# Up projections token-major, turned back through VectorE squares and DRAM

## The chip, the cores and the metric

One core of a Trainium2 chip runs the whole program. TensorE (PE) multiplies, VectorE (DVE) and ScalarE (ACT) do elementwise work, GpSimd (POOL) does little here, and the queues of SyncE (SP), ACT and POOL issue DMAs. The metric is device microseconds for one execution; the lower the better. A change of about 0.2% can be told from none.

## The reference

A decoder trunk of two layers over 256 tokens with D = 2048: a gated linear attention layer, then a block-sparse attention layer, each followed by the feed-forward block that the change touches:

```python
def conv_ffn(x, norm_w, w_up, conv_w, conv_b, w_down):
    h = rms_norm(x, norm_w) @ w_up              # (256, 2 * 5632)
    hp = jnp.pad(h, ((0, 0), (2, 0), (0, 0)))
    acc = conv_b
    for j in range(3):
        acc = acc + conv_w[j] * hp[:, j:j + S]  # causal, along the tokens, per feature
    a, u = jnp.split(acc, 2, axis=-1)
    return (jax.nn.silu(a) * u) @ w_down
```

All is float32.

## The kernel before

**Products.** A float32 product is made of three passes in the reduced type fp32r. Weights w are split into a high part (ACT's cast, line 132) and a low part (DVE's subtraction, line 133); the activations xw hold high and low parts side by side, 256 tokens each. A product is high x high, high x low and low x high, all summed in PSUM.

**Steps.** The program is an unrolled list of steps. In each step one 128x1024 piece of weights is taken from `WeightStream` and multiplied. `WeightStream` loads 128x2048 chunks (1 MB, three buffers `wraw`) through SP's queue (line 95) and splits them two steps or a little more ahead into three buffer pairs `whi`, `wlo`. `after(n, job)` puts a job n steps later into the program's order. Within each engine, the order is then settled by a scheduler at build time, which keeps dependencies and waits for buffers.

**Two forms of projection.** `gemm` is feature-major: weights stand in the array (128x128), the tokens stream. Per 128x128 weight tile it runs a matmul of 512 columns (high weights against high and low tokens, line 291) and one of 256 (low weights against high tokens, line 293). Its result has features on the partitions and tokens along the row. `gemm_tok` is token-major: 128 tokens stand in the array and 512 weight columns stream (lines 306 and 309). Its result has tokens on the partitions. The attention projections of the second layer use `gemm_tok`.

**The up stage** (`ffn`), for each of 44 tile pairs j (128 columns of a and the matching 128 of u): `gemm` in four steps, then `both` adds the two halves of the PSUM result (ACT line 319, DVE line 320), the row of norm factors `nrm.rstd` is multiplied in (line 593), and the convolution runs along the tokens (ACT line 597, DVE lines 599 and 601), then silu (line 603), the product (line 604) and the split into `hid` (lines 327 and 328). For some tile pairs (`EARLY`) the sums that the down projection wants are made at once (`combine`, lines 551 to 554); for others they are made in the down stage (`combine_parts`, line 561).

**The down stage** (`down`) runs a Strassen-like scheme: where its order list has a `+`, seven products take the place of eight, with weight sums (lines 105 to 107) and activation sums (`comb`). Its last entries (behind the `|`) are the tail.

**Buffers.** `slot` hands out 34 buffers of 4 KB a partition for xw (8), hid (22), combinations, weight sums and the rest.

**The norm.** `Norm.close` gives one factor per token with tokens on partitions (`col`); `spread` turns it into a row over tokens with a diagonal and two matmuls. `middle` makes the input of an up stage: `back` transposes the finished rows on PE.

Of the kernel before, what the change touches and what calls it, by code (L numbers as in the profile page):

```python
# [8 lines left out]
F32 = mybir.dt.float32  # L9
F32R = mybir.dt.float32r  # L10
I32 = mybir.dt.int32
AF = mybir.ActivationFunctionType
# [6 lines left out]
S = 256  # L19
KT = D // 128  # L20
# [7 lines left out]
FT = F // 128  # L28
# [3 lines left out]
C_GN, C_KVN, C_MN, C_FN, C_ON, C_KN, C_QN, C_CW = 0, 16, 32, 48, 80, 84, 85, 86  # L32
# [8 lines left out]
    return [(int(k.rstrip("+")), k.endswith("+")) for k in words], len(text.split("|")[1].split())  # L41


EARLY = (1, 3, 5, 7)
ORDERS = {
    "go": [_order("0 1+ 2 3+ 4 | 5 6 7"), _order("0 2 1+ 3+ 4 | 5 6 7")],
    "dn0": [_order("0 2 4 1+ 6 3+ 8 5+ 10 7+ 12 9+ 14 11+ 16 13+ 17 15+ 18 | 19 20 21"),
# [10 lines left out]
class WeightStream:  # L58
# [4 lines left out]
    def __init__(self, tc, raw, parts):  # L63
        self.tc, self.nc, self.raw, self.parts = tc, tc.nc, raw, parts
        self.chunks, self.halves = [], []
        self.tiles, self.split = {}, {}
        self.n_dma = self.n_split = 0
        self.cuts, self.lead, self.deep = {}, {}, set()
        self.sums, self.slot, self.first = {}, None, None
# [79 lines left out]
def trunk(ctx: ExitStack, tc: tile.TileContext, xT, x_tok, cst, msk, w1p, w2a, w_k, w_qa, w_v2, w_v, w_g, w_go,  # L149
          w_up0, w_dn0, w_kk, w_kv, w_mq, w_mo, w_up1, w_dn1, rel, onehot, out):  # L150
    nc = tc.nc
    V, A, T = nc.vector, nc.scalar, nc.tensor
# [6 lines left out]
    small = ctx.enter_context(tc.tile_pool(name="small", bufs=2))  # L159
    acc_ps = ctx.enter_context(tc.tile_pool(name="acc_ps", bufs=3, space=PSUM))  # L160
    mis_ps = ctx.enter_context(tc.tile_pool(name="mis_ps", bufs=2, space=PSUM))
    dram = ctx.enter_context(tc.tile_pool(name="dram", bufs=1, space=DRAM))
# [10 lines left out]
    def acc_pair():  # L173
# [2 lines left out]

    ws = WeightStream(tc, raw, parts)
    plan = [(w_v2, 1, 16384), (w_v, 2, 8192), (w_k, 4, 4096), (w_qa, 4, 4096), (w_g, 8, 4096), (w_go, "go", None),
            (w_up0, FT, 4096), (w_dn0, "dn0", None),
            (w_mq, 4, 8192), (w_kk, 4, 8192), (w_kv, 4, 8192), (w_mo, "mo", None),  # L180
            (w_up1, FT, 4096), (w_dn1, "dn1", None)]
    for w, groups, cols in plan:
        if cols is None:
            for g, order in enumerate(ORDERS[groups]):
# [49 lines left out]
    ident = mk[:, 0:128]  # L234
# [37 lines left out]
    def after(steps, job):  # L272
        later.append((cur[0] + steps, job))
# [10 lines left out]
    def gemm(xs, kts):  # L284
        ps = acc_ps.tile([128, 2, 512], F32, name="acc")
        for q0 in range(0, kts, 4):
            hi, lo = step()
            for bs in ((0,), (1,)) if q0 == kts - 4 else ((0, 1),):
                tiles_ = [(q0 + k, b, k * 256 + b * 128) for k in range(4) for b in bs]
                for kt, b, c in tiles_:  # L290
                    T.matmul(ps[:, b, :], hi[:, c:c + 128], xs(kt), start=kt == 0, stop=False)  # L291
                for kt, b, c in tiles_:
                    T.matmul(ps[:, b, :S], lo[:, c:c + 128], xs(kt)[:, :S], start=False, stop=kt == kts - 1)  # L293
        ws.prefetch(cur[0])
        return ps
# [21 lines left out]
    def both(ps, name):  # L317
        t = temp(name)
        A.copy(t, ps[:, :, S:])
        V.tensor_add(t, t, ps[:, :, :S])  # L320
        return t

    def bc(r):
        return r[:, None, :S].to_broadcast([128, 2, S])
# [5 lines left out]
    class Norm:  # L330


        def __init__(self, c, name, along=False):
            self.c, self.name, self.along, self.xs = c, name, along, []
            self.ss = small.tile([128, 2, 4], F32, name="ss_n")

        def operand(self, p, src):
# [5 lines left out]
        def close(self):  # L343
            m = small.tile([128, 2], F32, name="m_n")
            self.col = small.tile([128, 2], F32, name="col_n")
            V.tensor_reduce(m, self.ss, axis=AX.X, op=OP.add)
            V.tensor_scalar(m, m, 1.0 / D, EPS, op0=OP.mult, op1=OP.add)
            nc.gpsimd.tensor_tensor(self.col, m, mhalf[:, :2], op=OP.pow)

        def spread(self):  # L350

# [9 lines left out]
    nrm = Norm(C_GN, "xw")  # L361
# [9 lines left out]
    xs = rows(nrm.xs)  # L371
# [81 lines left out]
    for hd in (2, 3):  # L453
        ps = gemm_tok(xs)
# [9 lines left out]
    for hd in range(GH):  # L464
        ps = gemm(xs, KT)
        rstd = nrm.rstd
        k = both(ps, "k")
        V.tensor_mul(k, k, bc(rstd))
        b = bcum[hd]
# [64 lines left out]
    for hd in range(GH):  # L534
        ps = gemm(xs, KT)
        q = both(ps, "q")
# [10 lines left out]
    def combine(k, halves_, into):  # L547

        (a0, a1), (b0, b1) = halves_
        t = temp("comb", (128, 4, 128))  # L550
        V.tensor_add(t[:, 0], a1, b1)
        V.tensor_sub(t[:, 1], t[:, 0], a0)
        V.tensor_sub(t[:, 2], a0, a1)
        V.tensor_sub(t[:, 3], b0, t[:, 1])
        c = slot([128, 4, 2, 128], F32R, "comb")
        split(c[:, :, 0], c[:, :, 1], t)
        into[k] = c
# [10 lines left out]
    for hd in range(GH):  # L568
        for c in range(2):
            ps = gemm(xs, KT)  # L570
# [13 lines left out]
    def ffn(layer, nrm, then):  # L584
        xs = rows(nrm.xs)
        hid, sums = [], {}
        whole = [None, None]
        cw = C_CW + layer * 3 * 2 * FT
        cb = C_CB + layer * 2 * FT
        for j in range(FT):  # L590
            ps = gemm(xs, KT)
            t = both(ps, "up")
            V.tensor_mul(t, t, bc(nrm.rstd))  # L593
            au = temp("au")
            for i in range(2):
                n = i * FT + j
                A.activation(au[:, i, :], t[:, i, :], AF.Identity, bias=col(cb + n),  # L597
                             scale=col(cw + 2 * 2 * FT + n))
                V.scalar_tensor_tensor(au[:, i, 1:], t[:, i, :S - 1], col(cw + 2 * FT + n), au[:, i, 1:],
                                       op0=OP.mult, op1=OP.add)  # L600
                V.scalar_tensor_tensor(au[:, i, 2:], t[:, i, :S - 2], col(cw + n), au[:, i, 2:],  # L601
                                       op0=OP.mult, op1=OP.add)
            A.activation(au[:, 0, :], au[:, 0, :], AF.Silu)
            V.tensor_mul(au[:, 0, :], au[:, 0, :], au[:, 1, :])
            if j % 2 == 0:
                hid.append(slot([128, 2, 2 * S], F32R, "hid"))
            split(hid[-1][:, j % 2, :S], hid[-1][:, j % 2, S:], au[:, 0, :])
            whole[j % 2] = (au[:, 0, :128], au[:, 0, 128:])
            if j % 2 and j // 2 in EARLY:
                combine(j // 2, whole, sums)  # L610
        then(hid, sums)

    def down(name, xs, combos, res, done, jobs):
# [73 lines left out]
    def onward(nrm, keep_row, parked=None):  # L687

        sums = {}

        def done(t, c, x):
            sums[t, c] = x
            nc.gpsimd.dma_start(keep_row(t, c), x)
            nrm.square(t, c, x)

        def back(q, where):
            tp = where()
            for i in range(2):
                for t in range(2):
                    f = 128 * (q % 2 * 2 + i)  # L700
                    T.transpose(tp[:, i, 128 * t:128 * t + 128], sums[t, q // 2][:, f:f + 128], ident)  # L701
            nrm.operand(q, tp)
            if parked is not None:
                x = temp("hf")
                A.copy(x, tp)
                nc.gpsimd.dma_start(parked[q], x.rearrange("a b c -> a (b c)"))

        pair = []

        def in_acc():  # L710
            if not pair:
                pair.extend(acc_pair())
            return pair.pop(0)

        def in_bank():
            return bank("hf", (128, 2, S))

        return done, back, in_acc, in_bank

    def middle(name, xs, combos, res, nrm, keep_row, at, feature_major, parked=None):  # L720
        done, back, in_acc, in_bank = onward(nrm, keep_row, parked)
        jobs = {}
        for q, (b, i) in enumerate(at):
            jobs.setdefault(b, {}).setdefault(i, []).append(lambda q=q: back(q, in_acc))
        down(name, xs, combos, res, done, jobs)
        for q in range(len(at), NP):
            after(1 if feature_major else q - 3, lambda q=q: back(q, in_bank))
        after(2 if feature_major else 3, nrm.close)
        if feature_major:
            after(3, nrm.spread)  # L730

    rows1, rows2, rows3 = scratch("rows1"), scratch("rows2"), scratch("rows3")
    hspill = dram.tile([NP, 128, 2 * S], F32, name="hspill")
# [7 lines left out]

        down("dn1", hid, sums, rows3, done, {})

    n_ffn = Norm(C_FN, "xw")
    middle("go", go, go_sums, from_input, n_ffn, rows1, TURNS, True)
    n_q = Norm(C_MN, "xw")
    ffn(0, n_ffn, lambda hid, sums: middle("dn0", hid, sums, rows1, n_q, rows2,
# [120 lines left out]
    xs = rows(n_q.xs)  # L868
    for g in range(4):
        ps = gemm_tok(xs)  # L870
# [4 lines left out]
        f = (q8[:, g % 2 * 4:g % 2 * 4 + 4], (q1[:, 0:2], q1[:, 2:4]))  # L875
# [22 lines left out]
        for c in range(2):  # L898
            after(1 + c, lambda v=v, p=2 * g + c: values(v, p))

    n_ffn = Norm(C_FN + KT, "xw")
    middle("mo", ox, {}, rows2, n_ffn, rows3, TURNS, True)
    ffn(1, n_ffn, last_down)

# [1 line left out]
def _chunks(w):  # L906
    import numpy as np
    g, _, n = w.shape
    full = n // 2048 * 2048
    body = w[:, :, :full].reshape(g, 128, full // 2048, 2048).transpose(0, 2, 1, 3).reshape(g, -1)  # L910
    return np.ascontiguousarray(np.concatenate([body, w[:, :, full:].reshape(g, -1)], axis=1))


def _groups(w, width):
    k, n = w.shape
    return _chunks(w.reshape(k // 128, 128, n // width, width).transpose(2, 1, 0, 3)
                   .reshape(n // width, 128, -1))
# [20 lines left out]

def _pairs(w):
    k, n = w.shape  # L940
    j = n // 256
    return _chunks(w.reshape(k // 128, 128, 2, j, 128).transpose(3, 1, 0, 2, 4).reshape(j, 128, -1))


def _buckets():
# [64 lines left out]
```

## Time and profile before

| | |
|---|---|
| median of 3 runs | 2233.89 us (2233.52 to 2234.81) |
| profiled execution, span | 2230.9 us (for this execution the span is what the page states; the median lies 3.0 us above it) |
| PE / DVE / ACT busy | 2214.3 / 1663.1 / 1278.0 us |
| DMA | 441.07 MB, mean 198 GB/s; SP's queue 54.1% of the 16 engines |
| granted TensorE clock | 0.9 or more of full speed in every fortieth of the span |
| first up stage | PE's up matmuls from 387.3 to 881.0 us |

Busy time counts an engine's instructions from start to end; PE's matmuls overlap, so the distance between starts tells more than durations. A group row gives count, busy us, mean ns of one instruction, then idle time before it and what ended that idle time. A window row gives busy us (and instructions) of each engine within a stretch, the granted clock, the share of the 16 DMA engines and GB/s.

### The profile page before, as it was taken

The numbers are of one execution on the slowest core, as the hardware profiler recorded it, in microseconds if no ns is written. First come the engines' busy times: TensorE is split into PE (matmuls) and PEld (weight loads), VectorE is DVE, ScalarE is ACT, GpSimd is POOL, SyncE is SP. The second block draws the span as 40 slices with busy tenths as digits, with TensorE's granted clock in tenths as the row PEclk, the third lists the DMA queues.
The fourth block names the chain that finished last, engine by engine and source line by source line (L and its number), as shares of the span: only waits on it lengthen the run. The fifth ranks groups of instructions, "written<-read, shape, count | busy, mean of one in ns | idle before, by whom it ended". The sixth has DMA issues, their size and how long they took to land.

```text
span 2230.9 us, 30027 instructions
## 1 busy us (share of the span) xinstructions
PE 2214.3 (99%) x11525; PEld 1892.1 (85%) x11525; DVE 1663.1 (75%) x2305; ACT 1278.0 (57%) x1803; POOL 81.0 (4%) x104
## 2 busy tenths in 40 slices
PE   9999999999999999999999999999999999999999
PEld 7889887888888888888878888778888888888877
DVE  6566787777777778978766666677777777779786
ACT  6556655555555555655456665556555555556553
POOL 1000001000000000010030000010000000000000
PEclk9999999999999999999999999999999999999999
DMA  8553567555555555575675544575555555555755
GB/s 315 172 188 131 189 218 233 180 187 188 188 188 188 188 189 198 187 256 202 221 282 201 170 159 162 200 229 179 187 189 188 189 189 189 188 196 186 240 208 170
DMA packets 69777, 441.07 MB, mean 198 GB/s; under 512 B 8273, under 2 KB 8801, under 8 KB 19586
## 3 DMA queue, kind: packets, MB, share of 16 engines
q1 hardware_dynamic: 60578, 417.53, 54.1%
q0 software_dynamic: 8480, 21.05, 3.7%
q8 instruction: 90, 1.47, 0.3%
q10 hardware_dynamic: 576, 0.58, 0.1%
q14 instruction: 53, 0.43, 0.1%
HBM read 428.61 MB, written 10.51 MB: 197 GB/s over the span
## 4 chain that ended last, share of the span: by engine, by line
PE 96%; DMA 2%; DVE 2%; issue 0%; ACT 0%; SPq 0%; DVEq 0%; ACTq 0%
PE acc L291 34%; PE acc L293 18%; PE acc L639 16%; PE acc L306 10%; PE p L639 10%; PE acc L309 5%; DVE wlo L133 1%; DMA wraw<-w_dn 1%; PE sT L504 0%; DMA wraw<-w_v 0%; PE tr L793 0%; PE acc L701 0%; PE s L811 0%; PE pT L831 0%; DMA wraw<-w_mo 0%
## 5 line engine op out<-in xcount | busy, mean ns | idle before, releaser
L133 DVE TENSOR_TENSOR wlo<-wraw,whi 128x1024 fp32r<-128x1024 f32 (+1 forms) x786 | 929.9, 1191 | 395.2 <-ACT whi L132 373.2
L132 ACT CAST whi<-wraw 128x1024 fp32r<-128x1024 f32 (+1 forms) x786 | 798.8, 1026 | 690.4 <-PE acc L291 392.1
L291 PE MATMUL acc<-xw,whi 128*128 128x512 f32 x3328 | 853.9, 393 | 0.0
L291 PEld LDWEIGHTS acc<-xw,whi 128*128 128x128 f32 x3328 | 591.0, 189 | 99.0
L293 PEld LDWEIGHTS acc<-xw,wlo 128*128 128x128 f32 x3328 | 468.1, 190 | 41.8
L293 PE MATMUL acc<-xw,wlo 128*128 128x256 f32 x3328 | 481.5, 282 | 0.0
L639 PE MATMUL acc<-whi,hid 128*128 128x512 f32 x572 | 182.4, 390 | 0.7 <-DVE c L680 0.7
L639 PE MATMUL p<-whi,hid 128*128 128x512 f32 x506 | 166.1, 389 | 0.0
L306 PE MATMUL acc<-whi,xkv 128*128 128x512 f32 x512 | 133.6, 394 | 0.0
L306 PE MATMUL acc<-whi,xw 128*128 128x512 f32 x512 | 129.1, 392 | 3.0 <-ACT xw L244 1.5
L132 ACT CAST whi<-t 128x1024 fp32r<-128x1024 f32 x82 | 86.2, 1052 | 77.6 <-PE p L639 48.9
L639 PEld LDWEIGHTS acc<-whi,hid 128*128 128x128 f32 x572 | 107.0, 188 | 23.1 <-DVE c L680 1.1
L306 PEld LDWEIGHTS acc<-whi,xw 128*128 128x128 f32 x512 | 95.0, 188 | 24.7 <-ACT whi L132 2.8
L639 PE MATMUL acc<-whi,comb 128*128 128x512 f32 x328 | 107.5, 391 | 4.6 <-ACT whi L132 3.0
L639 PEld LDWEIGHTS p<-whi,hid 128*128 128x128 f32 x506 | 95.0, 188 | 19.8
L133 DVE TENSOR_TENSOR wlo<-t,whi 128x1024 fp32r<-128x1024 f32 x82 | 99.7, 1220 | 13.7 <-ACT whi L132 8.0
L306 PEld LDWEIGHTS acc<-whi,xkv 128*128 128x128 f32 x512 | 94.3, 188 | 18.4
L597 ACT ACTIVATE au<-up,cs 128x256 f32<-128x256 f32 x176 | 96.4, 595 | 20.0 <-DVE up L593 20.0
L639 PE MATMUL acc<-wlo,hid 128*128 128x512 f32 x286 | 94.7, 390 | 0.5 <-DVE wlo L133 0.5
L639 PE MATMUL p<-wlo,hid 128*128 128x512 f32 x253 | 83.5, 389 | 0.0
L601 DVE SCALAR_TENSOR_TENSOR au<-up,cs,au 128x254 f32<-128x254 f32 x176 | 77.4, 478 | 0.0
L639 PEld LDWEIGHTS acc<-whi,comb 128*128 128x128 f32 x328 | 61.5, 188 | 18.2 <-ACT whi L132 3.7
(261 smaller groups left out, 2062.8 us busy)
## 6 DMA issues: line engine op xcount, KB each, us to landing
wraw<-w_up SPq DMA_DIRECT2D x176, 1024.0 KB, 4.9
wraw<-w_dn SPq DMA_DIRECT2D x88, 1024.0 KB, 5.0
wraw<-w_g SPq DMA_DIRECT2D x16, 1024.0 KB, 4.9
wraw<-w_go SPq DMA_DIRECT2D x16, 1024.0 KB, 5.4
wraw<-w_mq SPq DMA_DIRECT2D x16, 1024.0 KB, 5.6
wraw<-w_kk SPq DMA_DIRECT2D x16, 1024.0 KB, 4.9
wraw<-w_kv SPq DMA_DIRECT2D x16, 1024.0 KB, 4.9
wraw<-w_mo SPq DMA_DIRECT2D x16, 1024.0 KB, 4.9
```

The lines of the kernel that those rows point to most:

```text
L132: nc.scalar.copy(hi[:, a:b], src[:, a:b])
L133: nc.vector.tensor_sub(lo[:, a:b], src[:, a:b], hi[:, a:b].bitcast(F32))
L291: T.matmul(ps[:, b, :], hi[:, c:c + 128], xs(kt), start=kt == 0, stop=False)
L293: T.matmul(ps[:, b, :S], lo[:, c:c + 128], xs(kt)[:, :S], start=False, stop=kt == kts - 1)
L306: T.matmul(ps[:, t, :], xs(kt)[:, x0 + 128 * t:x0 + 128 * t + 128], hi[:, c:c + 512], start=kt == 0 and x0 == 0, stop=False)
L309: T.matmul(ps[:, t, :], xs(kt)[:, 128 * t:128 * t + 128], lo[:, c:c + 512], start=False, stop=kt == KT - 1)
L597: A.activation(au[:, i, :], t[:, i, :], AF.Identity, bias=col(cb + n), scale=col(cw + 2 * 2 * FT + n))
L601: V.scalar_tensor_tensor(au[:, i, 2:], t[:, i, :S - 2], col(cw + n), au[:, i, 2:], op0=OP.mult, op1=OP.add)
L639: T.matmul(p[n], x[xi], w[wi][:, 512 * f:512 * f + 512], start=n not in begun, stop=left[n] == 0)
```

## The change

Both up stages go from `gemm` to `gemm_tok`: 22 groups J of 512 columns (a and u of two tile pairs) instead of 44 pairs of 256. The weights are laid out for it on the host. The result has tokens on the partitions, so it is turned back: ACT takes it out of PSUM with the norm factor of each token as scale; DVE transposes each 32x32 square; SP stores the squares to a DRAM scratch (one DMA of 512 KB, contiguous runs of 1 KB), and loads them with features on the partitions (four DMAs of 128 KB, runs of 256 B). The store stands one step after the group, the loads three, the two convolutions six and eight. To make that work the tokens of the normed input are interleaved when `back` transposes them (`is_woven`), and the norm column is permuted with eight small copies (`weave`), which stand in place of `spread`. The combination for tile 7 leaves `EARLY`.

```diff
-EARLY = (1, 3, 5, 7)
+EARLY = (1, 3, 5)
...
-            (w_up0, FT, 4096), (w_dn0, "dn0", None),
+            (w_up0, FT // 2, 8192), (w_dn0, "dn0", None),
...
+        def weave(self):
+            self.woven = small.tile([128, 2], F32, name="woven_n")
+            for t in range(2):
+                for i in range(4):
+                    q = 2 * (i % 2) + t
+                    A.copy(self.woven[32 * i:32 * i + 32, t:t + 1], self.col[32 * q:32 * q + 32, i // 2:i // 2 + 1])
...
-        for j in range(FT):
-            ps = gemm(xs, KT)
-            t = both(ps, "up")
-            V.tensor_mul(t, t, bc(nrm.rstd))
+        turned = dram.tile([FT // 2, 16, 32, 4, 64], F32, name=f"turned{layer}")
+
+        def square(J, ps):
+            z = slot([128, 16, 2, 32], F32, "z")
+            for t in range(2):
+                tok = temp("tok", (128, 512))
+                A.activation(tok, ps[:, t, :], AF.Copy, scale=nrm.woven[:, t:t + 1])
+                V.transpose(z[:, :, t, :], tok.rearrange("p (a b) -> p a b", b=32))
+            return z
+
+        def store(J, z):
+            nc.sync.dma_start(turned[J].rearrange("(a i) r q c -> (i r) a (q c)", a=4),
+                              z.rearrange("p (a q) t c -> p a (q t c)", a=4))
+
+        def load(J):
+            f = slot([128, 4, S], F32, "upT")
+            for q in range(4):
+                nc.sync.dma_start(f[32 * q:32 * q + 32].rearrange("p a (i c) -> p (a i) c", i=4),
+                                  turned[J][:, :, q, :].rearrange("a r c -> r a c"))
+            return f
+
+        def convolve(j, t):
             au = temp("au")
...
+        f = {}
+        for J in range(FT // 2):
+            ps = gemm_tok(xs)
+            z = square(J, ps)
+            after(1, lambda J=J, z=z: store(J, z))
+            after(3, lambda J=J: f.update({J: load(J)}))
+            for i in range(2):
+                after(6 + 2 * i, lambda J=J, i=i: convolve(2 * J + i, f[J][:, 2 * i:2 * i + 2, :]))
         then(hid, sums)
...
-                    T.transpose(tp[:, i, 128 * t:128 * t + 128], sums[t, q // 2][:, f:f + 128], ident)
+                    to = tp[:, i, 128 * t:128 * t + 128]
+                    if nrm.is_woven:
+                        to = tp[:, i, :].rearrange("p (t i c) -> p i t c", t=2, i=4)[:, 2 * t:2 * t + 2]
+                    T.transpose(to, sums[t, q // 2][:, f:f + 128], ident)
...
-            after(3, nrm.spread)
+            after(3, nrm.weave)
```

More of the change, by code (lines that the diff above doesn't have):

```diff
@@ L178, in trunk @@
     plan = [(w_v2, 1, 16384), (w_v, 2, 8192), (w_k, 4, 4096), (w_qa, 4, 4096), (w_g, 8, 4096), (w_go, "go", None),
-            (w_up0, FT, 4096), (w_dn0, "dn0", None),
+            (w_up0, FT // 2, 8192), (w_dn0, "dn0", None),
             (w_mq, 4, 8192), (w_kk, 4, 8192), (w_kv, 4, 8192), (w_mo, "mo", None),
-            (w_up1, FT, 4096), (w_dn1, "dn1", None)]
+            (w_up1, FT // 2, 8192), (w_dn1, "dn1", None)]
     for w, groups, cols in plan:
@@ L330, in trunk, with __init__ @@
     class Norm:
-        def __init__(self, c, name, along=False):
-            self.c, self.name, self.along, self.xs = c, name, along, []
+        def __init__(self, c, name, woven=False):
+            self.c, self.name, self.is_woven, self.xs = c, name, woven, []
             self.ss = small.tile([128, 2, 4], F32, name="ss_n")
@@ L742, in last_down @@
         down("dn1", hid, sums, rows3, done, {})
-    n_ffn = Norm(C_FN, "xw")
+    n_ffn = Norm(C_FN, "xw", True)
     middle("go", go, go_sums, from_input, n_ffn, rows1, TURNS, True)
@@ L899, in trunk @@
             after(1 + c, lambda v=v, p=2 * g + c: values(v, p))
-    n_ffn = Norm(C_FN + KT, "xw")
+    n_ffn = Norm(C_FN + KT, "xw", True)
     middle("mo", ox, {}, rows2, n_ffn, rows3, TURNS, True)
@@ L940, in _pairs @@
     k, n = w.shape
-    j = n // 256
-    return _chunks(w.reshape(k // 128, 128, 2, j, 128).transpose(3, 1, 0, 2, 4).reshape(j, 128, -1))
+    return _groups(w.reshape(k, 2, n // 256, 128).transpose(0, 2, 1, 3).reshape(k, n), 512)
 def _buckets():
```

## The prediction, made before the changed kernel was run

> **What bounds the kernel now.** I read the page first: its busy shares and the chain that ended last.
>
> ```profile
> span 2230.9 us, 30027 instructions
> PE 2214.3 (99%) x11525; PEld 1892.1 (85%) x11525; DVE 1663.1 (75%) x2305; ACT 1278.0 (57%) x1803; POOL 81.0 (4%) x104
> ...
> PE 96%; DMA 2%; DVE 2%; issue 0%; ACT 0%; SPq 0%; DVEq 0%; ACTq 0%
> ```
>
> PE carries 96% of the chain. So an edit pays by what it takes from PE's own stream, and costs by any moment at which it lets PE run dry. Next come the windows: a stretch of the first up stage, and one of the key projection, whose loop is already the token-major one (columns: length, PE, PEld, DVE, ACT, POOL busy, clock, DMA share, GB/s).
>
> ```profile
> 410.00:579.00 169.00, 169.00 (x969) 148.47 (x968) 131.25 (x201) 98.58 (x140) 0.00 (x0) 1.00 0.55 187
> 1200.00:1300.00 100.00, 100.00 (x482) 83.57 (x481) 68.91 (x115) 62.80 (x112) 9.73 (x4) 1.00 0.50 170
> ```
>
> Both have no PE gap, at full granted clock. The up stage can thus only gain if the same columns stream faster. A step is one 128x1024 weight tile, and in either form it streams 6144 columns: 8 matmuls of 512 and 8 of 256 today, 12 of 512 token-major. The chain and the matmul timeline give the length of a step (start, duration; a run's duration includes the drain of its last matmul, so I use starts):
>
> ```profile
> 411.32 1.84 PE acc L291 x8
> ...
> 579.12 1.84 PE acc L291 x8
> ```
> ```profile
> 402.76 2.02 PE L291 MATMUL acc<-xw,whi 128*128 128x512 f32 x8
> 404.62 1.11 PE L293 MATMUL acc<-xw,wlo 128*128 128x256 f32 x8
> 405.56 2.00 PE L291 MATMUL acc<-xw,whi 128*128 128x512 f32 x8
> ...
> 1231.96 1.98 PE L306 MATMUL acc<-whi,xkv 128*128 128x512 f32 x8
> 1233.77 1.07 PE L309 MATMUL acc<-wlo,xkv 128*128 128x512 f32 x4
> ...
> 1240.12 0.39 PE L306 MATMUL acc<-whi,xkv 128*128 128x512 f32 x1
> ```
>
> 579.12 - 411.32 is 167.80 us for 60 steps: 2.797 us a step now. Three token-major steps take 1240.12 - 1231.96 = 8.16 us: 2.720 us a step. The difference lies in the 256-column matmuls: 405.56 - 404.62 = 0.94 us for eight, 118 ns each, where half of a 512-column one (8.16/36 = 227 ns) is 113 ns.
>
> **The change part by part. 1. PE in the up stages.** There are 44 pairs of column tiles x 4 steps x 2 layers = 352 steps before, and 22 groups x 8 x 2 = 352 after. The gain is 352 x (2.797 - 2.720) = 27 us. This is the only large term, and it lies wholly on the path.
>
> [...]
>
> **2. Norm column instead of norm row.** The diagonal, its split and two 256-column matmuls per layer go: 2 x 118 ns x 2 layers, 0.5 us of PE. The eight 32x1 copies that come instead are priced by the last row of the next fence, 8 x 0.19 = 1.5 us of ACT per layer, first needed one whole group (21.8 us) later, with ACT busy 98.58/169 = 58%. Nothing. The transposes of the down results into interleaved columns keep their number and size; I price the new output pattern at nothing (between 0 and one more matmul slot of 0.1 us x 64 = 6 us; the strides are in PSUM, the stream stays 128 columns).
>
> **3. VectorE and ScalarE in a group** (mean ns is the second number behind the bar):
>
> ```profile
> L593 DVE TENSOR_TENSOR up<-up,rstd_h 128x512 f32<-128x512 f32 x88 | 60.8, 691 | 2.7
> L320 DVE TENSOR_TENSOR up<-up,acc 128x512 f32<-128x512 f32 x88 | 59.8, 680 | 0.0
> L319 ACT COPY up<-acc 128x512 f32<-128x512 f32 x88 | 51.0, 579 | 0.0
> L778 ACT ACTIVATE k<-acc,col_n 128x512 f32<-128x512 f32 x8 | 5.5, 692 | 0.0
> L599 DVE SCALAR_TENSOR_TENSOR au<-up,cs,au 128x255 f32<-128x255 f32 x176 | 76.9, 479 | 0.0
> L601 DVE SCALAR_TENSOR_TENSOR au<-up,cs,au 128x254 f32<-128x254 f32 x176 | 77.4, 478 | 0.0
> L604 DVE TENSOR_TENSOR au<-au 128x256 f32<-128x256 f32 x88 | 37.0, 420 | 1.3 <-ACT au L603 0.5
> L328 DVE TENSOR_TENSOR hid<-au,hid 128x256 fp32r<-128x256 f32 x88 | 36.9, 419 | 4.7 <-ACT hid L327 4.7
> L561 DVE TENSOR_TENSOR whole<-hid 128x512 f32<-128x512 f32 x9 | 6.2, 683 | 0.0
> L820 ACT ACTIVATION_READ_ACCUMULATOR s<-s,st 128x1 f32 x32 | 6.1, 192 | 0.0
> ```
>
> Per group of 512 columns, DVE loses 2 x (0.69 + 0.68) = 2.74 us (add, scale) and gains two 32x32 transposes. No row shows one; the nearest is any 128x512 pass, 0.68 us. Bounds: 0.35 (two elements at a time) to 1.4 us (half rate). I take 0.69, so +1.38. DVE now does 131.25/169 x 22.37 = 17.4 us per two pairs; after it 16.0 of 21.76 us (74%), at the upper bound 17.4 (80%). ACT loses 2 x 0.58 and gains 2 x 0.69: 13.05 to 13.3 us, 61%. Neither becomes the bound.
>
> **4. The round trip.** Per group one store of 512 packets of 1 KB and four loads of 512 packets of 256 B each, all on SP. Packet prices come from DMA answers cut to short windows: 0.5 to 4 us, where ACT's queue moved packets of 64 and 344 B, and the last 6.9 us, where it moved 2 KB packets (packets, MB, share of 16 engines):
>
> ```profile
> q10 hardware_dynamic: 285, 0.05, 7.7%
> ...
> q10 hardware_dynamic: 144, 0.26, 9.9%
> ...
> wraw<-w_up SPq DMA_DIRECT2D x176, 1024.0 KB, 4.9
> ...
> out_dram<-c SPq DMA_DIRECT2D x6, 256.0 KB, 2.2
> ```
>
> The first is 0.077 x 16 x 3.5 us / 285 = 15 ns at about 175 B, the second 0.099 x 16 x 6.9 / 144 = 76 ns at about 1.8 KB. Between them, 256 B costs 18 ns and 1 KB 46 ns. So a group adds 512 x 46 + 2048 x 18 = 60 engine-us to today's 0.55 x 16 x 22.37 = 197: 257 of 16 x 21.76 = 348, a share of 0.74. Bounds for the load packet: 15 and 76 ns, giving 0.72 and 1.08; I take the row of the small packets, which it is nearest to.
>
> On SP, a weight issue takes 0.33 us for 128 packets, and 0.38 for 256:
>
> ```profile
> L95 SPq DMA_DIRECT2D wraw<-w_up x176: 327/328/328, 365.6 to 1973.4; - x176
> ...
> L229 SPq DMA_DIRECT2D xt<-x_tok x4: 368/378/394, 17.5 to 23.8; - x4
> ```
>
> At that slope five issues of 512 packets take 5 x 0.48 = 2.4 us of SP's 21.76. What counts is the wait: the loads wait for the store to land (2.2 us for 256 KB, 4.9 us for 1 MB by the rows above: 3 to 5 us), and weight issues queue behind them. Their cover:
>
> ```profile
> 500.37 1.05 ACT L132 CAST whi<-wraw 128x1024 fp32r<-128x1024 f32 x1
> ...
> 503.93 1.22 DVE L133 TENSOR_TENSOR wlo<-wraw,whi 128x1024 fp32r<-128x1024 f32 x1
> ...
> 505.17 5.77 SPq L95 DMA_DIRECT2D wraw<-w_up  x2
> ```
>
> A weight buffer is taken from 500.37 to 505.15, refilled by about 510.1 (4.9 us), and wanted again three chunks later, 6 x 2.72 = 16.3 us after 500.37: 6.6 us of cover. An SP wait of 3 to 5 us once a group fits; loads ahead of the chunk in the engines (2048 x 18 / 16 = 2.3 us) bring it to the edge. I cost it at nothing, and at 1 us a group for each us beyond.
>
> **5. The convolution, 6 and 8 steps later.** From the group's last matmul: two activations and transposes, z complete by about 3 us, store landed by 6 to 8, loads landed 3 to 5 later: 9 to 13 us. The convolve stands at 16.3 us of PE time; ACT runs up to two steps ahead, so it may get there at 10.9. Waiting there, ACT holds the weight casts behind it, and VectorE their low parts; a cast is done two steps (5.4 us) before PE wants it, less its 1.05, so about 4 us more are covered. Cost nothing, with a thin margin.
>
> **6. What is moved into the down stage.** The last group's convolves, the second one of the group before, and the combination for tile 7 (no longer early) now fall at the head of the down stage. That is where DVE is full:
>
> ```profile
> 881.00:900.00 19.00, 19.00 (x86) 15.74 (x85) 18.07 (x34) 11.24 (x16) 0.00 (x0) 1.00 0.44 161
> 900.00:920.00 20.00, 20.00 (x90) 16.55 (x89) 19.77 (x27) 11.40 (x13) 0.00 (x0) 1.00 0.65 218
> 920.00:940.00 20.00, 20.00 (x90) 16.55 (x89) 18.16 (x20) 11.73 (x14) 0.00 (x0) 1.00 0.60 210
> 940.00:960.00 20.00, 20.00 (x90) 16.57 (x89) 18.76 (x20) 11.41 (x13) 0.00 (x0) 1.00 0.67 238
> ...
> 1998.00:2020.00 22.00, 22.00 (x99) 18.22 (x98) 21.66 (x39) 12.51 (x17) 0.00 (x0) 1.00 0.52 181
> 2020.00:2060.00 40.00, 40.00 (x178) 33.13 (x177) 37.87 (x45) 23.71 (x26) 0.00 (x0) 1.00 0.60 210
> ```
>
> DVE is 74.8 of 79 us busy there. A convolve costs it 2 x 0.48 + 2 x 0.48 + 0.42 + 0.42 = 2.8 us. Added: three of them (8.3), two transposes (1.4), the combination (about three 128x512 passes, 2.1): 11.8; gone: the last pair's 0.69 + 0.68 + 2.8 = 4.1. Net 7.7 us on 4.2 idle ones. Bounds per layer: 0 (the two-step lead swallows it) to 7.7. I take what exceeds the idle time of these rows, 3.5 us, 7 us for both layers. hid[21] itself is only wanted at the tail of the down order, so nobody waits for it.
>
> **Sum** against the profiled span: 2230.9 - 27 - 0.5 + 7 = 2210.4. The runs' median, 2233.9, is 3.0 us above the span: 2213.
>
> **The rivals.**
> A, the lead covers the down heads: 2213 - 7 = 2206. For it: PE is full in all six rows although DVE is at 95%. Against: no more than 4.2 us are free.
> B, they are wholly exposed: 2233.9 - 27.5 + 15.4 = 2222.
> C, slower: the loads land late, ACT stands at the convolve's first activation, the casts behind it are late and PE stops in each group. Place: ACT's queue, six steps behind a group. It decides when the landing is more than about 15 us after the group's last matmul; each further us costs 44 us, and 0.5 us a group (20.5/44) uses up the gain. At 1 us: 2213 + 44 = 2257. For it: 13 us is my upper estimate and SP takes its issues in order; against: the small-packet row and 26% free DMA time.
> D, the DMA engines become the bound: the load packet has to cost more than (348 - 197 - 24)/2048 = 62 ns; at 76 ns a group takes 376/16 = 23.5 us, 1.1 more than today: 2284 with 44 groups. The trace's 15 ns speaks against. [...]
> E, the 256-column matmul is no dearer than half a 512-column one, so the change of form gains nothing: 2233.9 - 0.5 + 7 = 2240; with only part of 7 us in the heads, no change. The 118 ns speak against it. [...]
>
> **How the numbers follow.** Forecast 0.38, A 0.28, B 0.12: all faster. C or D 0.13 slower; part of C using the gain up, 0.05 no change; E 0.04, half no change, half slower. A change of 0.2% (4.5 us) is what can be told here. Faster 0.78, same 0.07, slower 0.15. The likeliest case's own range is 2205 to 2222, by the bounds of 6. With 2 in 10 left out at most, the range goes from 2204 (the 27.5 us and a little) to 2231 (most of the gain used up).
>
> **What would show it.** Right: up-stage matmuls all of 512 columns, steps 2.72 us apart, PE without gaps; DVE transposes near 0.69 us; DMA share about 0.74 in the up windows; waits of VectorE's low parts in the first 80 us of each down stage, 3.5 us of PE. Wrong: convolve activations waiting for the loads and PE for the casts; weight casts waiting for DMA in the up stage; a step above 2.75 us without a wait.

## The result and the profile after

The changed kernel takes 2221.84 us (median of four, 2219.86 to 2226.41), the kernel before on the same chip 2233.7 (2232.66 to 2234.81): a ratio of 0.9948, 95% interval 0.9934 to 0.9962. It is faster by about half a per cent: a gain of 11.9 us, 9 less than forecast. The page of the profiled execution, in the lines that were shown of before:

```profile
span 2220.1 us, 27525 instructions
PE 2195.2 (99%) x10113; PEld 1824.6 (82%) x10113; DVE 1610.0 (73%) x2213; ACT 1280.0 (58%) x1815; POOL 82.2 (4%) x104
...
PE 94%; DVE 3%; DMA 2%; issue 1%; ACT 1%; SPq 0%; POOL 0%; DVEq 0%; ACTq 0%; POOLq 0%
```

PE still carries the chain, but its share fell from 96 to 94%, and VectorE's rose from 2 to 3%: somewhere PE now waits for VectorE. To find where, take the start of the first matmul of each stage from the matmul timeline (start, duration). For the attention input it is the first one behind the down stage's last product; in both kernels PE begins that stage's matmuls some 6 us earlier. First after, then before; the stages are up, down, attention input, attention output, up, down:

```profile
387.22 1.52 PE L306 MATMUL acc<-whi,xw 128*128 128x512 f32 x6
...
867.31 0.62 PE L674 MATMUL acc<-whi,hid 128*128 128x512 f32 x2
...
1108.84 0.62 PE L309 MATMUL acc<-wlo,xw 128*128 128x512 f32 x2
...
1401.78 0.61 PE L674 MATMUL acc<-whi,ox 128*128 128x512 f32 x2
...
1501.85 0.63 PE L306 MATMUL acc<-whi,xw 128*128 128x512 f32 x2
...
1981.96 0.62 PE L674 MATMUL acc<-whi,hid 128*128 128x512 f32 x2
```
```profile
387.31 1.52 PE L291 MATMUL acc<-xw,whi 128*128 128x512 f32 x6
...
881.00 0.63 PE L639 MATMUL acc<-whi,hid 128*128 128x512 f32 x2
...
1114.73 0.62 PE L309 MATMUL acc<-wlo,xw 128*128 128x512 f32 x2
...
1407.65 0.62 PE L639 MATMUL acc<-whi,ox 128*128 128x512 f32 x2
...
1503.26 2.00 PE L291 MATMUL acc<-xw,whi 128*128 128x512 f32 x8
...
1996.98 0.63 PE L639 MATMUL acc<-whi,hid 128*128 128x512 f32 x2
```

Differences of neighbouring rows give the ledger (the second down stage ends with the start of the last product, at 2226.70 before and 2215.55 after):

| stage | before, us | after, us | change | forecast |
|---|---|---|---|---|
| first up | 493.69 | 480.09 | -13.6 | -13.8 |
| first down | 233.73 | 241.53 | +7.8 | +3.5 |
| attention input | 292.92 | 292.94 | 0.0 | 0 |
| attention output | 95.61 | 100.07 | +4.5 | 0 |
| second up | 493.72 | 480.11 | -13.6 | -13.8 |
| second down | 229.72 | 233.59 | +3.9 | +3.5 |

The up stages gave what the forecast said. The down stages cost 11.7 us instead of 7, and a stage that the diff hardly touches costs 4.5 us.

**The up stages.** The chain of waits shows the length of a step (start, duration), and the windows show PE without a gap:

```profile
739.63 1.81 PE acc L306 x8
...
864.75 1.81 PE acc L306 x8
```
```profile
410.00:579.00 169.00, 169.00 (x748) 139.92 (x747) 121.95 (x181) 100.24 (x141) 0.00 (x0) 1.00 0.80 243
```

864.75 - 739.63 is 125.12 us for 46 steps: 2.720 us each, as in the key projection before. The groups of the new operations (mean ns is the second number behind the bar), the wait that ended most often at ACT (total us, times, longest), and the transfers (KB each, median us to landing):

```profile
L623 ACT ACTIVATE au<-upT,cs 128x256 f32<-128x256 f32 x176 | 95.8, 595 | 111.3 <-DMA upT<-turned 111.2
...
L605 DVE STREAM_TRANSPOSE z<-tok 128x512 f32<-128x512 f32 x88 | 57.3, 688 | 0.0
L604 ACT ACTIVATE tok<-acc,woven_n 128x512 f32<-128x512 f32 x88 | 55.4, 680 | 0.0
```
```profile
ACT au L623 <- DMA upT<-turned: 111.2, 39, 4.3
```
```profile
turned<-z SPq DMA_DIRECT2D x44, 512.0 KB, 3.1
upT<-turned SPq DMA_DIRECT2D x176, 128.0 KB, 5.7
```

The transposes take 0.69 us, the value taken. But ACT waits for the loads in 39 of 44 groups, 2.85 us on average, and PE does not feel it. One group of the up stage in full (timeline of after: start, duration, in brackets the idle time before and its releaser):

```profile
432.41 1.26 ACT L604 ACTIVATE tok<-acc,woven_n 128x512 f32<-128x512 f32 x2
...
438.36 2.14 SPq L615 DMA_DIRECT2D upT<-turned  x4
...
447.41 1.09 ACT L623 ACTIVATE au<-upT,cs 128x256 f32<-128x256 f32 x2 [4.03 <-DMA upT<-turned]
```

ACT stood ready 11 us after it took the group out of PSUM (447.41 - 4.03 - 432.41) and got the data after 15.0. Forecast were 10.9 and 9 to 13. So the loads are later than thought, and the 4 us of cover behind ACT are what saved the up stages.

**The head of the first down stage.** Windows, then the timeline of the same stretch:

```profile
867.00:887.00 20.00, 19.85 (x88) 15.99 (x87) 17.28 (x33) 11.87 (x19) 0.00 (x0) 1.00 0.84 267
887.00:907.00 20.00, 15.96 (x60) 11.85 (x60) 20.00 (x37) 10.31 (x15) 0.00 (x0) 0.91 0.23 89
```
```profile
870.62 0.38 SPq L609 DMA_DIRECT2D turned<-z  x1
...
877.62 2.05 SPq L615 DMA_DIRECT2D upT<-turned  x4
...
882.91 2.08 ACT L623 ACTIVATE au<-upT,cs 128x256 f32<-128x256 f32 x4 [4.00 <-DMA upT<-turned]
...
894.83 1.22 DVE L105 TENSOR_TENSOR t<-wraw 128x1024 f32<-128x1024 f32 x1
...
896.16 1.04 ACT L132 CAST whi<-t 128x1024 fp32r<-128x1024 f32 x1 [2.75 <-DVE t L105]
...
897.26 1.84 PE L674 MATMUL acc<-whi,comb 128*128 128x512 f32 x4 [2.92 <-ACT whi L132]
...
898.90 1.05 PE L674 MATMUL acc<-whi,hid 128*128 128x512 f32 x2
...
899.75 1.05 PE L674 MATMUL p<-whi,hid 128*128 128x512 f32 x2
```

The last group's data come 15.6 us after the stage began (882.91 - 867.31). Until then VectorE has 2.7 us idle out of 20: 1.8 end with ACT's late activation (at 883.55), 0.9 with the landing of a weight chunk (at 872.45). Then it has both last convolutions and the weight sums at once and is busy for the whole of the next 20 us. The weight sum of line 105, the second of the stage, stands behind the convolutions in VectorE's order and gets its turn only at 894.83; ACT's cast waits for it, and PE stands about 3.2 us. After the stop the matmuls start 0.41 to 0.43 us apart instead of 0.227 ((898.90 - 897.26)/4, (899.75 - 898.90)/2), some eight of them, which is another 1.6 us; the window's granted clock is 0.91. The second down stage has the same stop: 3.2 us until 2010.23, then 0.43 us from start to start.

### The profile page after: what moved, and what is told of

Read it like the earlier page. It is cut to its first block, busy times and chain, and to the rows that moved or that the text cites. A ratio compares the mean times of both kernels' runs of the same rounds, so it can differ in the third digit from the quotient of the medians.

```text
span 2220.1 us, 27525 instructions
## 1 busy us (share of the span) xinstructions
PE 2195.2 (99%) x10113; PEld 1824.6 (82%) x10113; DVE 1610.0 (73%) x2213; ACT 1280.0 (58%) x1815; POOL 82.2 (4%) x104
## 4 chain that ended last, share of the span: by engine, by line
PE 94%; DVE 3%; DMA 2%; issue 1%; ACT 1%; SPq 0%; POOL 0%; DVEq 0%; ACTq 0%; POOLq 0%
PE acc L306 39%; PE acc L309 19%; PE acc L674 15%; PE p L674 9%; PE acc L291 5%; PE acc L293 3%; DVE wlo L133 1%; DMA c<-rows 1%; PE sT L512 0%; ACT whi L132 0%; PE tr L831 0%; DMA wraw<-w_v 0%; PE acc L739 0%; DMA wraw<-w_mo 0%; PE s L849 0%
## 5 line engine op out<-in xcount | busy, mean ns | idle before, releaser
L306 PE MATMUL acc<-whi,xw 128*128 128x512 f32 x3328 | 825.2, 390 | 2.9 <-ACT xw L244 1.7
L306 PEld LDWEIGHTS acc<-whi,xw 128*128 128x128 f32 x3328 | 624.1, 188 | 133.6 <-ACT xw L244 2.9
L309 PE MATMUL acc<-wlo,xw 128*128 128x512 f32 x1664 | 445.5, 389 | 0.0
L309 PEld LDWEIGHTS acc<-wlo,xw 128*128 128x128 f32 x1664 | 312.2, 188 | 64.7
L623 ACT ACTIVATE au<-upT,cs 128x256 f32<-128x256 f32 x176 | 95.8, 595 | 111.3 <-DMA upT<-turned 111.2
L625 DVE SCALAR_TENSOR_TENSOR au<-upT,cs,au 128x255 f32<-128x255 f32 x176 | 79.2, 473 | 84.4 <-ACT au L623 84.0
L291 PE MATMUL acc<-xw,whi 128*128 128x512 f32 x512 | 132.6, 394 | 0.0
L674 PE MATMUL acc<-whi,comb 128*128 128x512 f32 x328 | 110.1, 400 | 10.9 <-ACT whi L132 9.3
L674 PEld LDWEIGHTS p<-whi,hid 128*128 128x128 f32 x506 | 95.5, 189 | 20.6 <-DVE c L715 0.6
L306 PEld LDWEIGHTS acc<-whi,xkv 128*128 128x128 f32 x512 | 94.3, 188 | 18.4
L291 PEld LDWEIGHTS acc<-xw,whi 128*128 128x128 f32 x512 | 90.8, 189 | 15.0
```

What stands on the lines that cost most here:

```text
L306: T.matmul(ps[:, t, :], xs(kt)[:, x0 + 128 * t:x0 + 128 * t + 128], hi[:, c:c + 512], start=kt == 0 and x0 == 0, stop=False)
L309: T.matmul(ps[:, t, :], xs(kt)[:, 128 * t:128 * t + 128], lo[:, c:c + 512], start=False, stop=kt == KT - 1)
L674: T.matmul(p[n], x[xi], w[wi][:, 512 * f:512 * f + 512], start=n not in begun, stop=left[n] == 0)
```

## The experiments

The theory formed from this: **the late load**. The last group's round trip ends late, VectorE loses time that it had, and the convolutions' work falls as a lump in front of the weight sums. The rival is the reason that the forecast gave: **the amount of work**, moved convolutions and the combination for tile 7, on a VectorE that is full.

**1. No round trip.** The squares are never stored or loaded; the convolutions read the buffer `z` as it is, so the values are not those of the reference. All VectorE and ACT work stays.

```diff
-            after(1, lambda J=J, z=z: store(J, z))
-            after(3, lambda J=J: f.update({J: load(J)}))
+            f[J] = z.rearrange("p a t c -> p (a t c)").rearrange("p (g s) -> p g s", g=4)
```

> Leaves out the store and the four loads: the convolutions read the transposed squares as they are (another order of the numbers, the same shapes and instructions). DVE and ACT work and their places unchanged. Theory 'late load': ACT's 111 us of waits for the load go, the stops in the down heads go, about 2212 us; up stages stay at 480.1 us each, since they were covered. Rival 'too much DVE work': the down heads stay as they are, 2219 to 2222 us.

Measured: 2212.63 us, ratio 0.9906 (0.9891 to 0.9921). Its windows at the same place:

```profile
867.00:887.00 20.00, 20.00 (x90) 16.54 (x90) 19.11 (x37) 13.62 (x21) 0.00 (x0) 1.00 0.49 168
887.00:907.00 20.00, 18.69 (x80) 14.53 (x79) 20.00 (x35) 10.07 (x14) 0.00 (x0) 1.00 0.47 168
```

VectorE now works 19.11 us in the first 20, not 17.28, and the largest stop is 1.1 us; the granted clock is 1.00 in both windows. Adding up what the distances between starts exceed 0.227 us by, where that is over 0.15 us, the down stages lose 1.7 us each, where the changed kernel lost 7.9 and 5.5. The up stages stay at 480.1 us: there, the round trip cost nothing. So the round trip is worth most of the loss in the down heads, with the amount of work the same: the two down stages take 465.8 us here, 475.1 in the changed kernel and 463.5 before.

**2. The combination for tile 7 early again.**

```diff
-EARLY = (1, 3, 5)
+EARLY = (1, 3, 5, 7)
-    big = ctx.enter_context(tc.tile_pool(name="big", bufs=34))
+    big = ctx.enter_context(tc.tile_pool(name="big", bufs=35))
```

> The changed kernel with the combination of tile 7 made early again (35 buffers in place of 34): about 2 us of DVE work per layer leave the down heads. Rival 'too much DVE work': 2 us less per layer, about 2218 us. Theory 'late load': ACT still waits 4 us for the load, the stop stays within 1 us, 2220 to 2222 us.

Measured: 2225.31 us, ratio 0.9963 (0.995 to 0.9976).

```profile
888.00:908.00 20.00, 15.96 (x55) 11.63 (x55) 19.97 (x35) 10.74 (x15) 0.00 (x0) 0.83 0.22 86
```

The stop of 3.2 us is still there in both down stages, at 899.1 and 2012.1, and the granted clock is lower still, 0.83 against 0.91. Less VectorE work in the head did not help: the rival is out as the main cause.

**3. Another queue for the round trip.** Store and loads are issued by POOL instead of SP.

```diff
-            nc.sync.dma_start(turned[J]...
+            nc.gpsimd.dma_start(turned[J]...
-                nc.sync.dma_start(f[32 * q:32 * q + 32]...
+                nc.gpsimd.dma_start(f[32 * q:32 * q + 32]...
```

> The changed kernel with the store and the four loads issued by POOL instead of SP, so that they no longer stand behind SP's weight chunks, nor the weight chunks behind them. Theory 'late load, late because of SP's queue': the loads land earlier, ACT's waits fall from 111 to under 60 us, the stops in the down heads shrink from 4.9 us to about 2 us, 2214 to 2217 us. Rival 'late because of the transfers themselves': the waits stay at 110 us or grow, 2220 us or more.

Measured: 2223.96 us, ratio 0.9958 (0.9943 to 0.9972). ACT's waits for the loads fell from 111.2 to 20.2 us over the program, and yet the kernel is no faster. (The same bytes go in fewer packets there, 14,784 more on POOL's queue for 116,160 fewer on SP's, so the run changes more than the place in a queue.) Timeline of the down head, whose first matmul is at 868.64:

```profile
879.18 2.59 POOL L615 DMA_DIRECT2D upT<-turned  x4 [4.58 <-DMA turned<-z]
...
887.02 2.08 ACT L623 ACTIVATE au<-upT,cs 128x256 f32<-128x256 f32 x4 [1.26 <-DMA upT<-turned]
...
898.48 2.07 PE L674 MATMUL acc<-whi,comb 128*128 128x512 f32 x4 [5.20 <-ACT whi L132]
```

The last group's data come 18.4 us after the stage began (887.02 - 868.64), 2.8 later than in the changed kernel, and the stop is 5.4 us instead of 3.2. Waits in the up stages are free; the one in the down head decides. With no trip, a trip of 15.6 and one of 18.4 us the largest stop is 1.1, 3.2 and 5.4 us. That is the late load's order, on three points.

**4. The last group's convolutions later: steps 12 and 14, and 34 and 36.** The two runs differ in the number.

```diff
-                after(6 + 2 * i, lambda J=J, i=i: convolve(...))
+                after((12 if J == FT // 2 - 1 else 6) + 2 * i, lambda J=J, i=i: convolve(...))
```

> The changed kernel, but the last group's two convolutions stand 12 and 14 steps after it instead of 6 and 8, so that their loads have landed when ACT gets there; the same work, still inside the first 80 us of the down stage, where DVE is full. Theory 'late load': the 3.2 us stop of PE some 30 us into each down stage (and the half-speed matmuls behind it) comes from ACT standing 4.0 us at the last group's convolution; both go, the down stages return from 235.4 and 233.6 us to about 229 and 230, the time to about 2212 us. Rival 'too much DVE work in the down head' (the step of the prediction): nothing is taken away, the stop stays, about 2220 to 2222 us.

> The same with lags of 34 and 36 steps: the last group's convolutions (5.6 us of DVE) leave the full stretch altogether. Theory 'late load': the same as with lag 12, about 2212 us. Rival 'too much DVE work': only now most of the stop goes, about 2212 us as well, and clearly below the kernel with lag 12.

Measured: 2217.89 us, 0.9931 (0.9914 to 0.9947), and 2218.07 us, 0.9932 (0.9917 to 0.9947). Both fall between the theories. With 12 the stop of 3.2 us is gone, and stops of 1.0 and 1.3 us stand in two places. Its timeline, in a down stage that begins at 868.36:

```profile
882.49 2.08 ACT L623 ACTIVATE au<-upT,cs 128x256 f32<-128x256 f32 x4 [4.01 <-DMA upT<-turned]
...
885.74 1.22 DVE L105 TENSOR_TENSOR t<-wraw 128x1024 f32<-128x1024 f32 x1
```

ACT meets the last group's load no later than in the changed kernel and waits the same 4.0 us for it. What differs is VectorE's order: the second weight sum now stands in front of the convolutions' second additions, 17.4 us into the stage. It starts 18.0 us into the stage before, 27.5 in the changed kernel, and 22.0, 27.2 and 27.4 us in experiments 1, 2 and 3; the largest stops there are 0, 3.2, 1.1, 3.2 and 5.4 us. So the late load alone is not enough: it costs the long stop where the build-time order has put the weight sum behind the work that waits for it.

With 34 the stops stand at 910.1 and 2019.7 (1.9 us). Its timeline:

```profile
898.07 1.09 ACT L623 ACTIVATE au<-upT,cs 128x256 f32<-128x256 f32 x2
```

Counted in the program's order, 34 steps reach some 60 us into the stage, whose steps are mostly shorter than 2.7 us (experiment 5 shows the place); the convolution runs 31 us into it. The build-time scheduler had pulled it forward, into the stretch where VectorE is full. So neither run moved the convolutions as far as its number says.

**5. The same, tied in place.** Steps 34 and 36, and the activations at the head of these convolutions are put behind the weight cast that ACT has issued last in that step.

```diff
-                    nc.scalar.copy(hi[:, a:b], src[:, a:b])
+                    self.last = nc.scalar.copy(hi[:, a:b], src[:, a:b]).ins
-                A.activation(au[:, i, :], t[:, i, :], AF.Identity, ...)
+                with tc.issue_after(ws.last) if j >= FT - 2 else nullcontext():
+                    A.activation(au[:, i, :], t[:, i, :], AF.Identity, ...)
-                after(6 + 2 * i, lambda J=J, i=i: convolve(...))
+                after((34 if J == FT // 2 - 1 else 6) + 2 * i, lambda J=J, i=i: convolve(...))
```

> The scheduler had put the last group's convolutions of the lag-34 kernel some 28 us after the group all the same, in the full stretch; here they are tied behind the weight cast of their step, so that they really run 90 us later. Theory 'an idle DVE for the late load, and 5.6 us of lumped convolution work, cause the stops in the down heads': both are away, the two down stages return to 229 and 230 us, the time to about 2213 us. Rival 'DVE is overfull there by the combination of tile 7 alone': 1 to 2 us of stops remain per layer, 2215 to 2217 us.

Measured: 2209.11 us (2208.35 to 2210.37), ratio 0.9887 (0.987 to 0.9903): the fastest version here, below both kernels.

```profile
867.00:887.00 20.00, 20.00 (x90) 16.54 (x89) 18.15 (x34) 11.27 (x15) 0.00 (x0) 1.00 0.78 245
887.00:907.00 20.00, 19.92 (x88) 16.20 (x87) 19.45 (x29) 10.34 (x12) 0.00 (x0) 1.00 0.49 180
907.00:927.00 20.00, 19.56 (x87) 15.87 (x86) 19.72 (x22) 13.13 (x15) 0.00 (x0) 1.00 0.61 225
```
```profile
929.39 1.09 ACT L624 ACTIVATE au<-upT,cs 128x256 f32<-128x256 f32 x2
```

The last convolutions now run 61 us into the stage (it began at 867.93), where some 90 were expected. VectorE is busy for none of these stretches in full, PE loses 0.8 and 0.5 us in the two down stages, and the clock stays at 1.00. The round trip is as late as before (ACT still waits 104.7 us for loads in 36 groups); only nobody stands behind it in the down head. The work is the same too. Nor is it the weights' own landing: VectorE waits 2.4 us for a chunk of weights in this head (until 887.55), longer than the 0.9 us in the changed kernel, and PE goes on. With experiments 1 and 4: the long stop came of two things together, the late load and a weight sum that stands behind the convolutions on VectorE; without either of them it is gone.

**6. Tied in place, with tile 7 early** (edits of 2 and 5 together).

> The same with the combination of tile 7 made early again (35 buffers). DVE's work in the down heads is then below that of the kernel before. Theory of the lump: no gain over the pinned kernel, 2212 to 2214 us. Rival 'combination of tile 7': 2 to 4 us less than the pinned kernel, about 2212 where that one shows 2216.

Measured: 2212.92 us, ratio 0.9904 (0.9889 to 0.9919); 3.8 us slower than version 5 on the same chip. The two down stages have a stop of 1.5 us each, at 951.5 and 2057.6. Taking this work out of the down head gained nothing again.

**7. The convolutions two steps earlier, everywhere** (a test of rival C: the load is late, ACT stands, PE stops in each group).

```diff
-                after(6 + 2 * i, lambda J=J, i=i: convolve(...))
+                after(4 + 2 * i, lambda J=J, i=i: convolve(...))
```

> The changed kernel with the convolutions 4 and 6 steps after their group instead of 6 and 8: ACT meets the loads two steps (5.4 us) earlier. Rival C of the prediction (late loads stop PE in each group beyond about 4 us of cover) says: ACT's mean wait grows from 2.9 to about 8 us, some 4 us beyond the cover, 22 x 4 = 90 us more in each up stage, about 2400 us. Against it: the scheduler settles ACT's order by its own estimate of the landing; if it keeps the casts in front, the up stages stay near 480 us and the time near 2222.

Measured: 2289.54 us (2283.9 to 2296.35), ratio 1.0254 (1.0231 to 1.0276). The chain of releasers among its waits:

```profile
ACT au L623 <- DMA upT<-turned: 236.2, 44, 8.0
...
PE acc L306 <- ACT whi L132: 46.3, 32, 3.0
```

ACT's wait grew from 2.85 to 5.4 us a group (236.2/44), not to the 8 expected, and the up stages from 480.1 to 508.2 and 512.4 us, 1.4 us a group. If every further us of waiting costs PE one, the cover behind ACT is 5.4 - 1.4 = 4.0 us: the 4 us of the prediction's part 5. Rival C's mechanism is real, and begins on average about 1.2 us (4.0 - 2.85) beyond where the change stands.

**8. The instruction stream shifted**, for the attention output. In its slow place the chunks of weights landed after 6.9 us (median of two) instead of 4.9, with one packet of instruction loading among the transfers. Here 26 matmuls without use stand at the start of the program instead of 8, 24 of them of 128 columns instead of 512.

> The changed kernel with 26 short warm-up matmuls at the start in place of 8 long ones: PE's instruction stream shifts by 36 instructions, the work does not. Theory 'code load': the attention output stage, not touched by the change, took 100.1 instead of 95.6 us because a 16 KB instruction packet (1.7 us) falls on the one weight chunk that ACT waits for there; shifted by about 4 us it misses the chunk, the stage returns to 95.5 to 97 us, the time falls by 3 to 4.5 us to about 2218. Rival 'the change itself makes the stage longer' (another place in memory, another order): it stays at 99 to 100 us, 2221 to 2222 us.

Measured: 2222.54 us, ratio 0.9952 (0.9938 to 0.9967). The instruction packet has gone from that place, the chunks land after 5.7 us, and the pause behind them is 1.1 us, not 1.5. The stage takes 98.8 us instead of 100.1, not the 95.5 to 97 expected; without the shift, versions 1 to 7 take 97.5 to 99.6 us there, version 1 without any round trip 99.4. So no gain of the shift can be told from chance. Windows of this stage, first this run's, then those of after and of before:

```profile
1403.00:1503.00 100.00, 94.92 (x419) 77.43 (x418) 70.55 (x82) 50.96 (x74) 11.52 (x16) 0.97 0.68 219
```
```profile
1402.00:1502.00 100.00, 93.95 (x413) 76.51 (x412) 69.99 (x80) 50.33 (x69) 11.00 (x15) 0.97 0.67 217
```
```profile
1407.00:1504.00 97.00, 92.04 (x420) 75.14 (x419) 70.98 (x83) 51.53 (x71) 10.99 (x15) 1.00 0.69 225
```

The clock is 0.97 with and without the packet, and 1.00 before. Of the 4.5 us, 1.5 are longer pauses of PE (6.7 against 5.2 us in the pauses over half a microsecond), and the rest, 3.0 us, goes with half-speed matmuls behind them, 0.43 us from start to start for 512 columns. Instruction loading explains at most 0.4 us of them.

Versions 5 and 6 have the same pause of 1.5 us in this stage, ending at 1408.1 and 1410.0, and the stage of 6 is 2.05 us shorter (97.51 against 99.56). Windows of 3.41 us show why, first of 5, then of 6:

```profile
1405.22:1408.63 3.41, 1.89 (x8) 0.90 (x6) 3.40 (x5) 1.29 (x3) 0.00 (x0) 1.00 0.23 46
1408.63:1412.04 3.41, 3.36 (x12) 2.99 (x12) 0.00 (x0) 0.12 (x1) 0.00 (x0) 0.50 0.63 262
```
```profile
1405.87:1409.28 3.41, 2.78 (x11) 1.53 (x9) 3.41 (x6) 2.02 (x3) 0.00 (x0) 1.00 0.08 31
1409.28:1412.69 3.41, 2.44 (x13) 2.04 (x14) 1.29 (x3) 0.72 (x2) 0.00 (x0) 1.00 0.83 288
1412.69:1416.11 3.42, 2.05 (x13) 1.42 (x11) 2.52 (x4) 2.64 (x5) 0.00 (x0) 1.00 0.05 19
```

In the changed kernel the granted clock is halved four times between 25 and 2200 us, each time for 3.41 us: from 897.56, 1416.39, 1471.00 and 2010.31. These starts lie whole multiples of 3.413 us apart: 152, 16 and 158 such stretches. The windows above are cut on a grid of this length (that of 6 is counted on from a halved stretch at 357.98). In 5 the whole pause falls into one stretch, PE is busy for 1.89 us of it, and the next runs at 0.50. In 6 the grid divides the pause, PE is busy for 2.78 and 2.44 us, and the clock stays at 1.00. In the changed kernel PE was busy for 0.49, 1.62, 1.58 and 0.49 us of the stretches just before the halved ones, and for 1.78 us of the emptiest one that no halved one follows (354.84 to 358.25). In the kernel before it was busy for 2.01 us of the emptiest one here (1424.32 to 1427.73), and the clock was not halved between 25 and 2200 us. So 5 and 6, with a pause of the same length, differ in where it falls on the grid, which no edit here controlled. Why the pauses themselves are longer in the changed kernels stays open.

## Why the prediction was right, and where not

1. **PE in the up stages**: right. Steps of 2.720 us, 27.2 us saved against 27.5 with the norm. Rival E is refuted: it was right to let the 118 ns of the 256-column rows decide.
2. **The norm**: nothing of it can be seen by itself; the up stages' sum leaves no room for a cost.
3. **VectorE and ScalarE in a group**: right. 0.69 and 0.68 us; VectorE is busy 121.95 of 169 us, 72%, where 74% were forecast.
4. **The round trip**: hidden, as forecast, but two sizes were too small. The DMA share is 0.80, not 0.74. With 197 + 24 engine-us for weights and store, a load packet costs (0.80 x 348 - 221)/2048 = 28 ns by this estimate, not 18: the row of ACT's small packets did not carry over. (The packets' own durations in the trace, between 410 and 860 us, average 27.7 ns for the 256 B and 47 ns for the 1 KB ones.) And the four loads took 9.0 us from the first issue to the last landing in the group shown, where 3 to 5 were reckoned. Rival D's 62 ns stayed far.
5. **The convolution**: "cost nothing, with a thin margin" held for the up stages, and the cover of 4 us was measured. The landing was wrong: 15.0 us after ACT began to take the group out, outside 9 to 13. On average about 1.2 us of margin were left.
6. **The down heads**: the term that was mis-sized, 11.7 us for 7, and with a wrong cause. The prediction weighed VectorE's added work against its idle time over 80 us. That work was 5.5 us more in the first down stage (busy 192.16 before, 197.62 after), not 7.7, and alone it leaves 1.7 us of pauses a layer (experiment 1) and, spread out, less than 1 (experiment 5); before there were 0.9 and 1.6. What cost the rest is when it came: part 5's late load keeps VectorE idle for 1.8 us, then the convolutions stand in front of the weight sum, and PE's stop is followed by half-speed matmuls. The late landing does not hold up PE in 21 of a layer's 22 groups; the prediction did not follow it to the last, where VectorE has no idle time to make up for it.
7. **Not foreseen**: 4.5 us in the attention output, a third of it longer pauses, the rest the clock, halved for two stretches of 3.41 us (from 1416.39 and 1471.00) where before it was not.

The measured terms sum to -27.2 + 11.7 + 4.5 = -11.0 us, and the spans differ by 10.8. That rival B's 2222 lies beside the result is chance: B put 15.4 us into the down heads. The direction and the large term were right by their mechanism; that 2221.84 still lies inside the range owes something to the range's width, for it is the edge of the likeliest case's own (2205 to 2222), and 4.5 us of the shortfall come from a stage priced at nothing.

## What to carry to other kernels

When a change adds a latency that the steady state hides, follow the last item of the pipeline into the next stage: there the cover is another one, and the deferred work can arrive in a lump on an engine that may be full. Look there for what stands behind it in that engine's order. Sum an engine's load over stretches of the size of the lead of its consumers, not over the whole stage: a sum of 95% over 80 us did not show the 20 us without a gap. And a move in the program's order is only made when the schedule shows it: read in the timeline where the instruction really went, and tie it down if it went elsewhere.

## What the runs showed of the hardware that was not expected

- After stops of PE some matmuls ran at half speed. In the down head of the changed kernel, behind the stop of 3.2 us, eight of them started up to 0.43 us apart with 512 columns, not 0.227, which added 1.6 us, about half the price of the stop. The granted clock was 0.50 for 3.41 us behind the 1.5 us of version 5, and 0.83 over the 20 us with the 5.4 us stop of experiment 3.
- The half speed came in stretches of 3.41 us, which began 152, 16 and 158 such stretches apart in the changed kernel. A pause of the same length (1.5 us) was followed by one in version 5, where it left PE busy for 1.89 us of one stretch, and not in version 6, where the grid divided it (2.78 and 2.44 us).
- Packets of 256 B, read from DRAM in their thousands, took 27.7 ns of a DMA engine each on average (changed kernel, 410 to 860 us), about twice the 15 ns that the prediction estimated from the small packets in the profile of before.
